# Stores on GpSimd's queue, late sums in single steps, five early down steps, and each product's high parts first, in a layer of HGRN2, RWKV-7 and a ConvFFN

## The chip, the cores and the metric

One core of a Trainium2 chip runs the whole layer. The metric is the device time of one execution in microseconds; the median of the runs counts.

## The reference

Input and output are (1, 2048, 1024) in float32. The layer, cut to what matters:

```python
h = _rmsnorm(x, norm1_w)
proj = h @ w_in                                  # 1024 -> HGRN2 and RWKV-7 columns
o_hg = _hgrn2_mixer(...); o_rw = _rwkv7_mixer(...)
x = x + concat([o_hg, o_rw]) @ w_out
u = _rmsnorm(x, norm2_w) @ w_up                  # 1024 -> 2 * 2816
u = causal_depthwise_conv(u, width=3) + conv_b
gate, val = split(u, 2)
x = x + (silu(gate) * val) @ w_down              # 2816 -> 1024
return _rmsnorm(x, final_norm_w)
```

The change lies behind the two mixers: in the end of the output projection, the up projection, and the down projection.

## The kernel before

The time axis (2048) is cut into four blocks of 512. **Stage 1** runs norm, input projection, both mixers and most of the output projection. **Stage 2** begins at about 1390 us of the span and has three parts.

*Operands in two parts.* Each float32 operand is split into a high and a low part: ScalarE (ACT) casts (L245 in `split`, L238 in `split_to`), VectorE (DVE) subtracts (L246, L239). A product is three matmuls of 128x128 by 128x512 in `mm3` (L261 high by high, L262 and L263 with a low part each), summed in one PSUM bank. In the names, a final h or l is the part: `uwh`, `uwl`, `Bh`, `Bl`, `dah`, `dal`.

*The end of the output projection (1390 to 1440 us, tile `wacc`).* The last block, two halves of 512 columns with eight steps `n` of four tiles each. The results are added to the residual and stored to `x1d` in DRAM (SP's queue). Beside it the first operands of the up stage are built: `br` tiles are loaded and split into `Bh`, `Bl`.

*The up stage (1440 to 2338 us, tiles `ua`, `ub`, `ud`).* The up product uses seven products of half-size blocks instead of eight, so sums of operands are needed on both sides: of weights (`weight_sums`), of activations (`Ts`), for the down stage of its weights (`Tw`) and of its inputs (`Sg`). The function `run` goes over 44 iterations n, 22 (`NFF`) for each half h of the time axis. An iteration has seven calls of `prod`, each 12 matmuls: a11, a12, s2, s1, s3, and a22 and s4, which run late, within the next iteration. ACT copies three sums out of PSUM as `m` (L117, `part`), and `ua` can't be written again before; DVE finishes the columns (convolution, gate, `y`) and SP stores them to `gd` (L1447). At the end of the first half, `between` adds one product of the down stage (tile `fa`, 11 steps of 12 matmuls), a step behind most calls of `prod` in n = 21 and 22.

*Side jobs.* `side` is a list of small jobs in a written order; `aside(n)` takes one after each product, if the job's first iteration (`first_at`) has come. `norm_last` normalizes the second half's blocks, `four` makes four sums of four loaded `br` tiles (a ring of six): load, nothing, two operations, two operations and four stores, nothing. For `Sg` of the second group (g = 1) the kk-th set starts at iteration 35 + kk, 8 of 11 sets (`EARLY`); the other three are made in the down stage by `g_sums`.

*The down stage (2338 to 2731 us, tiles `da`, `db`).* 143 steps (g, p, kk) of 12 matmuls. The first three are made at the up stage's end by `down_start`, called between the last s4 product and the rest of `late`, with `br`/`uw` tiles; then a new pool opens, whose operands `draw` are loaded by `load`, four steps ahead, and split by `take`, two ahead. Residual tiles of 512 KB (`xt`, L1473) and the last norm's weights (`fw`) are loaded in between. Finished rows go out to `out` (L1489).

A list scheduler orders each engine's instructions; the order below is its result, before and after. DMAs are issued by SP or by GpSimd (POOL): each is a queue with an order of its own, in which a transfer that waits for its data holds up those behind it.

Of the kernel before, what the change touches and what calls it, by code (L numbers as in the profile page):

```python
# [18 lines left out]
P = 128  # L19
# [42 lines left out]
def tile_layer(ctx, tc, consts, x, norm1_w, w_in, hg_lb_logits, hg_norm_w, rw_shift_mu, rw_w0, rw_w2,  # L62
# [5 lines left out]
    dma = nc.sync.dma_start  # L68
# [112 lines left out]
    EARLY = 8  # L181
# [10 lines left out]
    def g_sums(tile_, g, kk):  # L192

        a11, a12, a21, a22 = (tile_(krows(gd_[2 * g + u], q, kk)) for u in range(2) for q in range(2))
        V.tensor_add(a22, a21, a22)
        V.tensor_sub(a21, a11, a21)
        V.tensor_sub(a11, a22, a11)
        V.tensor_sub(a12, a12, a11)
        for i, t_ in enumerate((a22, a11, a21, a12)):
            dma(krows(Sg[g][i], 0, kk), t_)  # L200
# [7 lines left out]
    def d_loads(s_, tile_):  # L208
        g, p, kk = steps[s_]
        _, a, b = DP[p]  # L210
        return (tile_(krows(Sg[g][a], 0, kk) if isinstance(a, int) else krows(gd_[2 * g + a[0]], a[1], kk)),
                tile_(krows(Tw[b], 0, kk) if isinstance(b, int) else wd_quarter(*b, kk)))

# [45 lines left out]
    def mm3(acc, lhs, rhs, first, last, skip=False):  # L259
        (lh, ll), (rh, rl) = lhs, rhs  # L260
        TE.matmul(acc, lh, rh, start=first, stop=False, skip_group_check=skip)  # L261
        TE.matmul(acc, lh, rl, start=False, stop=False, skip_group_check=skip)  # L262
        TE.matmul(acc, ll, rh, start=False, stop=last, skip_group_check=skip)  # L263

# [843 lines left out]
    with ExitStack() as c2:  # L1108
# [36 lines left out]
        with tc.tile_pool(name="op", bufs=1, reuse_waits="tile") as op_:  # L1145
# [52 lines left out]
            for dh in range(2):  # L1198
                accs = [pst("wacc") for _ in range(4)]
                for n, k in enumerate((0, 1, 4, 5, 2, 3, 6, 7)):  # L1200
                    w = weights(k, dh)
                    if dh == 0:
                        take(k)
                    if n == 5:
                        for i in range(4):
                            t0 = b * BLK + i * P
                            if dh:
                                x_tile(i)
                            load(xt[i], x[0, t0:t0 + P, dh * 512:dh * 512 + 512])
# [12 lines left out]
                    for i in range(4):  # L1222
                        is_ = slice(i * P, (i + 1) * P)
                        mm3(accs[i], (ohl[k][0][:, is_], ohl[k][1][:, is_]), w, n == 0, n == KD - 1)
                for i in range(4):
                    V.tensor_add(xt[i], accs[i], xt[i])
                    dma(x1d[b][i * P:(i + 1) * P, dh * 512:dh * 512 + 512], xt[i])


        with tc.tile_pool(name="up", bufs=1, reuse_waits="tile") as up:  # L1230
# [11 lines left out]
            def norm_last(b, i2):  # L1242
# [11 lines left out]
                def evict(k, tp, w):  # L1254
                    t_ = hr.tile([P, 256], F32, tag="br", name="h2", bufs=6)
                    act(t_, tp, AF.Copy, scale=w)
                    dma(h2d[b][k * P:(k + 1) * P, i2 * 256:i2 * 256 + 256], t_)
# [4 lines left out]
            def four(srcs, make, dsts):  # L1262

                ts = []
                aside_of([lambda: ts.extend(raw_(v) for v in srcs), None,
                          lambda: make(ts, 0), lambda: (make(ts, 1), [dma(d, t_) for d, t_ in dsts(ts)]), None])
# [10 lines left out]
            def s_make(ts, part):  # L1277
                a11, a12, a21, a22 = ts
                if part == 0:
                    V.tensor_add(a22, a21, a22)  # L1280
                    V.tensor_sub(a21, a11, a21)
                else:
                    V.tensor_sub(a11, a22, a11)
                    V.tensor_sub(a12, a12, a11)
# [3 lines left out]
            s_out = lambda row: lambda ts: [(row(i), ts[j]) for i, j in enumerate((3, 0, 2, 1))]  # L1288
# [21 lines left out]
            def down_start():  # L1310

                accs = [pst("da") for _ in range(4)]
                raws = [d_loads(s_, raw_) for s_ in range(3)]
                for s_ in range(3):
                    lhs, rhs = (split(uw, t_, [P, BLK], "uw", 5) for t_ in raws[s_])
                    for i in range(4):
                        d_matmuls(accs, s_, lhs, rhs, i)
                dstate["accs"] = accs

            def between():  # L1320

                accs = [pst("fa") for _ in range(4)]
                for kk in range(KH):
                    lhs, rhs = (split(uw, raw_(v), [P, BLK], "uw", 5)
                                for v in (krows(gd_[0], 1, kk), wd_quarter(1, 0, kk)))
                    for i in range(4):
                        mm3(accs[i], [t_[:, i * P:(i + 1) * P] for t_ in lhs], rhs, kk == 0, kk == KH - 1, True)
# [3 lines left out]
                for i in range(4):  # L1331
                    t_ = raw_(None)
                    act(t_, accs[i], AF.Copy)
                    dma(M2[i], t_)
# [9 lines left out]
            def run():  # L1344
# [9 lines left out]
                for n in range(2 * NFF + 1):  # L1354
                    h, fb = n // NFF, n % NFF
                    if n < 2 * NFF:
# [7 lines left out]
                        def prod(acc, nm, bi, first, n=n, ops=ops):  # L1364
# [4 lines left out]
                            for k in range(4):  # L1369
                                mm3(acc, (wh[:, k, :], wl[:, k, :]), (bh[:, k, :], bl[:, k, :]),  # L1370
                                    first and k == 0, k == 3, True)
# [26 lines left out]
                    if n == 2 * NFF:  # L1398
                        break
# [22 lines left out]
                    def late(h=h, fb=fb, operand=operand, prod=prod, acc_a=acc_a, acc_d=acc_d, a22=a22, a12=a12, cg=cg,  # L1422
# [23 lines left out]
                        for b in range(2):  # L1446
                            (dma if end is None else nc.gpsimd.dma_start)(gd_[2 * h + b][fb * P:(fb + 1) * P, :],  # L1447
# [5 lines left out]
    with tc.tile_pool(name="dn", bufs=1, reuse_waits="tile") as dn:  # L1453
# [11 lines left out]

        def load(s_):
# [18 lines left out]
        def finish(g, u, i):  # L1485
# [3 lines left out]
            dma(out[0, t0:t0 + P, :], t_)  # L1489
# [16 lines left out]
        for s_ in range(3, 7):  # L1506
            load(s_)
        take(3)
        take(4)
# [3 lines left out]
        for s_ in range(3, N):  # L1513
# [6 lines left out]
            if s_ < N - 3:  # L1520
                lhs, rhs = ops.pop(s_)
                for i in range(4):
                    d_matmuls(acc, s_, lhs, rhs, i)
                    if kk == KH - 1:
# [50 lines left out]
```

## Time and profile before

| | us |
|---|---|
| runs | 2748.82, 2748.41, 2739.77 (median 2748.41) |
| profiled execution | 2740.67 |
| its span | 2738.9 |
| TensorE busy in the span | 2634.9 (96%) |
| VectorE, ScalarE, GpSimd busy | 1896.9, 1344.5, 367.4 |

A row of waits reads: engine, line and tile that waited, the engine, tile and line it waited for, us in total, times, longest. A row of DMA issues: out<-in, queue, number, KB each, median us from issue to landing. A row of the timeline: start, length, engine, line, operation, out<-in. A matmul's length is modelled and overlaps the next one's, so the pace is read from the starts. PE is TensorE, SPq and POOLq are the queues of SP and GpSimd.

### The profile page before, as it was taken

Reading aid. Unit: us, or ns where it says so; the run is one execution under the profiler, and the core shown is the slowest. Engines: PE = TensorE matmul, PEld = TensorE weight load, DVE = VectorE, ACT = ScalarE, POOL = GpSimd, SP = SyncE. Lnnn points to the kernel's source line nnn. Section 1 sums busy time; section 2 is a strip of 40 time slices with the busy share of each in tenths; the row PEclk is TensorE's granted clock in tenths of the full one; section 3 lists DMA queues with packets and bytes.
Section 4 is the critical chain, followed back from the end, with each engine's and each line's share of the span. In section 5 each row is a group of like instructions: output and inputs, shape, how many; then the busy total and the mean of one; then the engine's idle time right before and its main releaser. Section 6 shows DMA issues by size and latency. Waiting matters only on the chain.

```text
span 2738.9 us, 47949 instructions
## 1 busy us (share of the span) xinstructions
PE 2634.9 (96%) x18059; PEld 2098.9 (77%) x18059; DVE 1896.9 (69%) x3665; ACT 1344.5 (49%) x2168; POOL 367.4 (13%) x660
## 2 busy tenths in 40 slices
PE   7999999989999999999899999999999999999998
PEld 6777777767777767777677788887888877788887
DVE  4857656566556664656667889988898888667556
ACT  5446443444544444334456754556545444445444
POOL 6433222212321113222100000000000000000000
PEclk9999999999999999999999999999999999999999
DMA  8655544355663546844575357746763454888665
GB/s 302 200 159 165 165 138 128 115 152 164 216 189 105 152 137 208 273 142 133 168 260 179 118 197 265 237 151 208 259 223 123 145 185 151 285 303 273 214 193 185
DMA packets 365438, 517.87 MB, mean 189 GB/s; under 512 B 97440, under 2 KB 194070, under 8 KB 365206
## 3 DMA queue, kind: packets, MB, share of 16 engines
q1 hardware_dynamic: 313265, 345.39, 39.3%
q0 software_dynamic: 51872, 169.41, 19.0%
q8 instruction: 142, 2.33, 0.3%
q14 instruction: 91, 0.74, 0.1%
q10 hardware_dynamic: 68, 0.02, 0.0%
HBM read 376.27 MB, written 138.41 MB: 188 GB/s over the span
## 4 chain that ended last, share of the span: by engine, by line
PE 67%; DMA 10%; DVE 10%; issue 6%; ACT 4%; SPq 1%; POOL 1%; DVEq 0%; ACTq 0%; POOLq 0%
PE pj L261 8%; PE pj L262 7%; PE pj L263 7%; PE ua L261 4%; PE ua L263 4%; PE ua L262 4%; PE da L262 2%; PE da L261 2%; PE da L263 2%; PE ud L263 2%; PE ud L261 2%; PE ud L262 2%; PE db L262 2%; PE db L263 2%; PE hg L972 2%
## 5 line engine op out<-in xcount | busy, mean ns | idle before, releaser
L261 PE MATMUL pj<-hh,wh 128*128 128x512 f32 x960 | 403.2, 420 | 2.3 <-ACT hh L117 1.4
L263 PE MATMUL pj<-hh,wl 128*128 128x512 f32 x960 | 380.0, 396 | 0.1
L262 PE MATMUL pj<-hl,wh 128*128 128x512 f32 x960 | 379.1, 395 | 0.0
L261 PE MATMUL ua<-Bh,uwh 128*128 128x512 f32 x704 | 277.0, 393 | 10.4 <-ACT m L117 9.3
L263 PE MATMUL ua<-Bh,uwl 128*128 128x512 f32 x704 | 274.5, 390 | 0.1
L262 PE MATMUL ua<-Bl,uwh 128*128 128x512 f32 x704 | 274.2, 390 | 0.0
L261 PEld LDWEIGHTS pj<-hh,wh 128*128 128x128 f32 x960 | 181.7, 189 | 55.4 <-issue 12.7
L263 PEld LDWEIGHTS pj<-hh,wl 128*128 128x128 f32 x960 | 181.5, 189 | 40.8 <-DMA wl<-Win170l 0.9
L262 PEld LDWEIGHTS pj<-hl,wh 128*128 128x128 f32 x960 | 181.8, 189 | 39.6 <-issue 6.2
L245 ACT CAST uwh<-uraw 128x512 fp32r<-128x512 f32 x220 | 133.2, 616 | 101.5 <-PE ua L262 42.0
L246 DVE TENSOR_TENSOR dal<-draw,dah 128x512 fp32r<-128x512 f32 x140 | 96.7, 690 | 116.0 <-ACT dah L245 115.4
L245 ACT CAST dah<-draw 128x512 fp32r<-128x512 f32 x140 | 87.1, 622 | 169.9 <-PE da L262 81.6
L246 DVE TENSOR_TENSOR uwl<-uraw,uwh 128x512 fp32r<-128x512 f32 x220 | 146.8, 686 | 31.3 <-ACT uwh L245 31.1
L261 PEld LDWEIGHTS ua<-Bh,uwh 128*128 128x128 f32 x704 | 132.2, 188 | 41.8 <-ACT m L117 14.0
L263 PEld LDWEIGHTS ua<-Bh,uwl 128*128 128x128 f32 x704 | 132.2, 188 | 28.7 <-DVE uwl L246 1.0
L262 PEld LDWEIGHTS ua<-Bl,uwh 128*128 128x128 f32 x704 | 132.3, 188 | 26.6
L261 PE MATMUL ud<-Bh,uwh 128*128 128x512 f32 x352 | 137.8, 391 | 0.0
L263 PE MATMUL ud<-Bh,uwl 128*128 128x512 f32 x352 | 137.1, 389 | 0.0
L262 PE MATMUL ud<-Bl,uwh 128*128 128x512 f32 x352 | 137.0, 389 | 0.0
L261 PE MATMUL da<-dbh,dah 128*128 128x512 f32 x340 | 131.2, 390 | 3.4 <-ACT dbh L245 3.4
L262 PE MATMUL da<-dbl,dah 128*128 128x512 f32 x340 | 132.5, 390 | 0.5 <-DVE dbl L246 0.5
L263 PE MATMUL da<-dbh,dal 128*128 128x512 f32 x340 | 132.1, 389 | 0.0
(570 smaller groups left out, 6049.5 us busy)
## 6 DMA issues: line engine op xcount, KB each, us to landing
uraw<-in_w_up_dram SPq DMA_DIRECT2D x176, 256.0 KB, 3.2
woraw<-in_w_out_dram POOLq DMA_DIRECT2D x96, 256.0 KB, 3.6
br<-gd SPq DMA_DIRECT2D x90, 256.0 KB, 4.4
draw<-Sg SPq DMA_DIRECT2D x88, 256.0 KB, 3.2
draw<-Tw SPq DMA_DIRECT2D x88, 256.0 KB, 3.5
gd<-y SPq DMA_DIRECT2D x86, 256.0 KB, 3.0
Sg<-br SPq DMA_DIRECT2D x76, 256.0 KB, 2.5
xt<-x1d SPq DMA_DIRECT2D x32, 512.0 KB, 6.7
```

The source lines that it names most:

```text
L245: S.copy(hi, src)
L246: V.tensor_sub(lo, src, hi.bitcast(F32))
L261: TE.matmul(acc, lh, rh, start=first, stop=False, skip_group_check=skip)
L262: TE.matmul(acc, lh, rl, start=False, stop=False, skip_group_check=skip)
L263: TE.matmul(acc, ll, rh, start=False, stop=last, skip_group_check=skip)
L972: TE.matmul(o, kt[:, t0:t0 + 64], qs, start=True, stop=True, tile_position=(0, e * 64))
```

## The change

Four edits. (1) `store` is GpSimd's queue: the stores of x1d, h2d, Ts, Tw, Sg, gd, M2 and the first group's output move there from SP's, 286 in all; SP's program goes from 1339 to 1053 instructions and GpSimd's from 664 to 950. (2) The sums `Sg` have seven jobs: load, two empty, then one operation and its store each; the second group's sets start at iteration 36 + kk, and 7 of them instead of 8 are made in the up stage. (3) `down_start` makes five steps (`DS`) instead of three, and loads each step's operands in turn, not all ahead; the residual loads of p = 0 move from kk = 4, 6, 8, 10 to 5, 6, 8, 9. (4) `terms3` orders 12 matmuls as four high by high, then four of each low part, in `prod`, `between`, the down steps but each p's last, and the first two of the eight steps of the projection; before, each tile's three followed one another. TensorE's and VectorE's numbers of instructions stay as they were.

```diff
-    dma = nc.sync.dma_start
+    dma, store = nc.sync.dma_start, nc.gpsimd.dma_start
...
-    EARLY = 8
+    DS = 5
+    EARLY = 7
...
+    def terms3(jobs, first, last):
+
+        for j in range(3):
+            for n, (acc, (lh, ll), (rh, rl)) in enumerate(jobs):
+                TE.matmul(acc, *((lh, rh), (lh, rl), (ll, rh))[j], start=first(n) and j == 0, stop=last(n) and j == 2,
+                          skip_group_check=True)
...
-                    dma(x1d[b][i * P:(i + 1) * P, dh * 512:dh * 512 + 512], xt[i])
+                    store(x1d[b][i * P:(i + 1) * P, dh * 512:dh * 512 + 512], xt[i])
...
+            def sums(g, kk):
+
+                ts = []
+                ops = ((3, V.tensor_add, 2, 3), (2, V.tensor_sub, 0, 2), (0, V.tensor_sub, 3, 0), (1, V.tensor_sub, 1, 0))
+
+                def op(d, f, a, b, i):
+                    f(ts[d], ts[a], ts[b])
+                    store(krows(Sg[g][i], 0, kk), ts[d])
+
+                aside_of([lambda: ts.extend(raw_(krows(gd_[2 * g + u], q, kk)) for u, q in QB), None, None]
+                         + [lambda o=o, i=i: op(*o, i) for i, o in zip((0, 2, 1, 3), ops)])
+
             for g in range(2):
-                for kk in range(({0: KH, 1: EARLY})[g]):
-                    first_at[0] = NFF + 1 + g * (KH + 1 + kk)
-                    four([krows(gd_[2 * g + u], q, kk) for u, q in QB], s_make,
-                         s_out(lambda i, g=g, kk=kk: krows(Sg[g][i], 0, kk)))
+                for kk in range((KH, EARLY)[g]):
+                    first_at[0] = NFF + 1 + g * (KH + 2 + kk)
+                    sums(g, kk)
...
-                raws = [d_loads(s_, raw_) for s_ in range(3)]
-                for s_ in range(3):
-                    lhs, rhs = (split(uw, t_, [P, BLK], "uw", 5) for t_ in raws[s_])
-                    for i in range(4):
-                        d_matmuls(accs, s_, lhs, rhs, i)
+                for s_ in range(DS):
+                    lhs, rhs = (split(uw, t_, [P, BLK], "uw", 5) for t_ in d_loads(s_, raw_))
+                    d_step(accs, s_, lhs, rhs)
...
-                            (dma if end is None else nc.gpsimd.dma_start)(gd_[2 * h + b][fb * P:(fb + 1) * P, :],
+                            store(gd_[2 * h + b][fb * P:(fb + 1) * P, :],
...
-                if p == 0 and kk in (4, 6, 8, 10) or p == 2 - g and kk in (1, 3, 5, 7):
-                    u, i = (0, kk // 2 - 2) if p == 0 else (1, kk // 2)
+                if p == 0 and kk in XT or p == 2 - g and kk in (1, 3, 5, 7):
+                    u, i = (0, XT.index(kk)) if p == 0 else (1, kk // 2)
```

**VectorE, in one iteration of the late sums (g = 1).** The additions and subtractions of `br` tiles are the four operations of a set (L1280 to L1284 before, L1308 after); `uwl` are low parts of weights, `y`, `cg`, `cv` the finishing of columns. Before:

```order
L246 TENSOR_TENSOR uwl_22111<-s1_22086,uwh_22110 128x512
L1280 TENSOR_TENSOR br_22013<-br_22011,br_22013 128x512
L1281 TENSOR_TENSOR br_22011<-br_22007,br_22011 128x512
L246 TENSOR_TENSOR uwl_22134<-uraw_21986,uwh_22133 128x512
L1283 TENSOR_TENSOR br_22007<-br_22013,br_22007 128x512
L1439 SCALAR_TENSOR_TENSOR y1_22057<-cv_21895,cvt_14639,y1_22057 128x1024
L1431 TENSOR_TENSOR cg_21894<-ud_21897,m2_21937 128x512
L1440 SCALAR_TENSOR_TENSOR y1_22057<-cv_21895,cvt_14639,y1_22057 128x1024
L1284 TENSOR_TENSOR br_22009<-br_22009,br_22007 128x512
```

After, from the last operation of one set to the third of the next:

```order
L1434 TENSOR_TENSOR cv_21716<-ud_21718,m3_21791 128x512
L1308 TENSOR_TENSOR br_21822<-br_21822,br_21820 128x512
L1451 COPY cg_21878<-halo_15086 128x2
L1451 COPY cv_21879<-halo_15086 128x2
L252 TENSOR_TENSOR uwl_21922<-s1_21899,uwh_21921 128x512
L1308 TENSOR_TENSOR br_22067<-br_22065,br_22067 128x512
L1308 TENSOR_TENSOR br_22065<-br_22061,br_22065 128x512
L252 TENSOR_TENSOR uwl_21941<-uraw_21799,uwh_21940 128x512
L1308 TENSOR_TENSOR br_22061<-br_22067,br_22061 128x512
L1454 SCALAR_TENSOR_TENSOR y1_21870<-cv_21716,cvt_14639,y1_21870 128x1024
```

The first operation stays at the same place of an iteration, while the last one stands 21 rows behind the first instead of 4 to 7, in the next iteration.

**TensorE, at the end of the up stage.** `ud` is the last s4 product, `da` with `uw` operands the early down steps, `da` with `dbh`, `dah` the first step from the new pool. Before, there are 31 early matmuls from the last `ud` to that step, of which these rows are the first and the last:

```order
L263 MATMUL ud<-Bh_15084,uwl 128x512
L263 MATMUL da<-uwh,uwl 128x512
L261 MATMUL da<-uwh 128x512
L262 MATMUL da<-uwl,uwh 128x512
```

```order
L263 MATMUL da<-uwh,uwl 128x512
L261 MATMUL da<-dbh,dah 128x512 x4
```

After, 14 rows of four stand there, 56 matmuls; the first six of them and the row ahead:

```order
L275 MATMUL ud<-Bh_15084,uwl 128x512 x4
L275 MATMUL da<-uwl,uwh 128x512 x4
L275 MATMUL da<-uwh,uwl 128x512 x4
L275 MATMUL da<-uwh 128x512 x4
L275 MATMUL da<-uwl,uwh 128x512 x4
L275 MATMUL da<-uwh,uwl 128x512 x4
L275 MATMUL da<-uwh 128x512 x4
```

Two more steps stand ahead of the new pool's first operand, and the parts come in fours.

**ScalarE, in the first iteration of the up stage.** `m1` is the copy that frees `ua`; the casts to `Bh6`, `Bh2` wait for loads of `br`, the one to `uwh` for a load of weights (`uraw`). Before:

```order
L238 CAST Bh5_14664<-br_15137 128x512
L117 ACTIVATE m1_15153<-ua_15088 128x512
L238 CAST Bh6_14658<-br_15159 128x512
L238 CAST Bh6_14658<-br_15163 128x512
L238 CAST Bh6_14658<-br_15167 128x512
L238 CAST Bh6_14658<-br_15171 128x512
L117 ACTIVATE m2_15216<-ua_15088 128x512
```

After:

```order
L244 CAST Bh5_14664<-br_15137 128x512
L244 CAST Bh6_14658<-br_15167 128x512
L244 CAST Bh6_14658<-br_15171 128x512
L244 CAST Bh2_15084<-br_15188 128x512
L251 CAST uwh_15260<-uraw_15251 128x512
L117 ACTIVATE m1_15153<-ua_15088 128x512
L244 CAST Bh2_15084<-br_15192 128x512
```

`m1` moves behind four casts of `Bh6` (two stand just ahead of these rows), one of `Bh2` and one of weights.

More of the change, by code (lines that the diff above doesn't have):

```diff
@@ L212, in d_loads, with d_step @@
                 tile_(krows(Tw[b], 0, kk) if isinstance(b, int) else wd_quarter(*b, kk)))
+    def d_step(accs, s_, lhs, rhs):
+        g, p, kk = steps[s_]
+        terms3([(accs[i], [t_[:, i * P:(i + 1) * P] for t_ in lhs], rhs) for i in range(4)],
+               lambda i: kk == 0 and p in (0, 1, 3), lambda i: False)
     def d_matmuls(accs, s_, lhs, rhs, i):
@@ L1488, in finish @@
             t0 = (2 * g + u) * BLK + i * P
-            dma(out[0, t0:t0 + P, :], t_)
+            (dma if g else store)(out[0, t0:t0 + P, :], t_)
         def evict(g, p, accs, i):
@@ L1505, in tile_layer @@
         accs = {"a": dstate["accs"]}
-        for s_ in range(3, 7):
+        for s_ in range(DS, DS + 4):
             load(s_)
-        take(3)
-        take(4)
+        take(DS)
+        take(DS + 1)
         fw = dn.tile([P, D], F32, name="fw")
@@ L1512, in tile_layer @@
         sums_at = {KH + 6 * j + 2: EARLY + j for j in range(KH - EARLY)}
-        for s_ in range(3, N):
+        for s_ in range(DS, N):
             g, p, kk = steps[s_]
@@ L1521, in tile_layer @@
                 lhs, rhs = ops.pop(s_)
[L1522 to L1524 removed]
+                if kk < KH - 1:
+                    d_step(acc, s_, lhs, rhs)
+                else:
+                    for i in range(4):
+                        d_matmuls(acc, s_, lhs, rhs, i)
                         evict(g, p, accs, i)
```

37 lines of the change are left out of this document (16 added, 21 removed).

## The prediction

> **What bounds the kernel now.** I read the page first, then the busy time by stretches, then TensorE's waits in each stretch, then the queues behind those waits.
>
> ```profile
> span 2738.9 us, 47949 instructions
> PE 2634.9 (96%) x18059; PEld 2098.9 (77%) x18059; DVE 1896.9 (69%) x3665; ACT 1344.5 (49%) x2168; POOL 367.4 (13%) x660
> ```
>
> TensorE is busy nearly throughout. Stage 1 (to about 1390 us) keeps its order of instructions on every engine, so only what lies behind it can move.
>
> ```profile
> core 0: us, PE busy (x) PEld busy (x) DVE busy (x) ACT busy (x) POOL busy (x), PEclk, DMA share, GB/s
> 1390.00:1440.00 50.00, 47.55 (x203) 38.58 (x202) 36.47 (x59) 25.06 (x43) 0.63 (x1) 0.97 0.91 304
> 1440.00:2338.00 898.00, 882.53 (x3898) 723.22 (x3897) 771.04 (x1168) 492.21 (x752) 0.00 (x0) 1.00 0.58 188
> 2338.00:2731.00 393.00, 388.95 (x1708) 319.70 (x1707) 245.63 (x369) 188.01 (x341) 1.10 (x2) 1.00 0.73 242
> 1560.00:1700.00 140.00, 140.00 (x630) 115.27 (x629) 122.69 (x194) 78.33 (x124) 0.00 (x0) 1.00 0.65 213
> 2191.00:2331.00 140.00, 133.01 (x579) 108.25 (x580) 115.94 (x169) 66.76 (x100) 0.00 (x0) 1.00 0.52 169
> ```
>
> The rows are the last block's output projection, the up stage, the down stage, a clean piece of the up stage and its late piece. The granted clock is full from 1440 us on. TensorE stands still for 2.45 us in the first, 15.47 in the second and 4.05 in the third, 22.0 together; in the clean piece not at all. Its pace where nothing waits:
>
> ```profile
> 1619.69 0.39 PE L261 MATMUL ua<-Bh,uwh 128*128 128x512 f32 x1
> ...
> 1622.18 0.39 PE L263 MATMUL ua<-Bh,uwl 128*128 128x512 f32 x1
> 1622.41 0.39 PE L261 MATMUL ud<-Bh,uwh 128*128 128x512 f32 x1
> ...
> 1624.90 0.39 PE L263 MATMUL ud<-Bh,uwl 128*128 128x512 f32 x1
> ```
>
> 24 starts, 23 steps, 5.21 us: 0.2265 us from matmul to matmul, though each lasts 0.39 (they overlap). The step from L263 to L261 at 1622.18, where weights, moving operand and accumulator all change, is 0.23 like the others. So the second half of the change, another order of the same matmuls, has no pace to win or lose; it can only move the moment at which an operand is needed. And a wait costs more than the idle time shown, since the last matmul's end (0.39) was counted as busy where 0.23 would have done: idle time plus 0.16 a wait. The waits, for the output projection, for 1395 to 2340 us, and for 2340 to 2740:
>
> ```profile
> PE wacc L263 <- DVE Bl L239: 1.3, 1, 1.3
> PE wacc L262 <- DVE wol L239: 1.1, 1, 1.1
> ```
>
> ```profile
> PE ua L261 <- ACT m L117: 9.3, 8, 1.7
> PE fa L262 <- DVE uwl L246: 3.0, 2, 1.9
> PE fa L261 <- ACT uwh L245: 1.0, 1, 1.0
> PE ua L261 <- ACT uwh L245: 1.0, 1, 1.0
> PE tp L255 <- DVE xt L1252: 1.0, 1, 1.0
> ```
>
> ```profile
> PE da L261 <- ACT dbh L245: 3.4, 3, 1.5
> PE da L262 <- DVE dbl L246: 0.5, 2, 0.2
> PE db L262 <- DVE dbl L246: 0.2, 1, 0.2
> ```
>
> They add up to 2.4 + 15.3 + 4.1 = 21.8 us in 21 waits; with 21 x 0.16 = 3.4 that is **25 us, the most that stage 2 can give** without taking matmuls out, and the instruction counts are unchanged.
>
> **The change part by part.**
>
> *The late sums (7.1 us of the 9.3).* From 2185 to 2336 us the waits of TensorE, VectorE and SP's queue are
>
> ```profile
> PE ua L261 <- ACT m L117: 7.1, 6, 1.6
> ```
>
> ```profile
> DVE br L1280 <- DMA br<-gd: 19.0, 6, 3.9
> ```
>
> ```profile
> SPq L1447 <- DVE y L1445: 25.3, 8, 16.5
> SPq L1266 <- DVE br L1280: 23.4, 6, 4.7
> SPq L1266 <- DVE br L1284: 9.3, 3, 3.1
> ```
>
> Read from the bottom: SP stands 58 us at stores whose data aren't there; the loads of br behind them, which wait for gd besides, go out late; VectorE stands 19.0 us at the first sum with its other work queued behind; ACT's copy m comes late, and the next product on ua waits. The change cuts this in three places: the stores leave SP; the sums of the second group start one iteration later (84 matmuls, 19.0 us); and the four operations get a slot each, the last one 21 rows behind the first in VectorE's order instead of 4 to 7. Nothing then stands between br's landing and its use but the ring of six buffers: 6 x (1.18 + 0.16) = 8.1 us. I take **8.0**; bounds 0 and 8.1. One set fewer is done here and one more in the down stage, where VectorE is free a third of the time (245.63 of 393 busy).
>
> *Stores, price.* Landing times, all at 256 KB:
>
> ```profile
> gd<-y SPq DMA_DIRECT2D x86, 256.0 KB, 3.0
> Sg<-br SPq DMA_DIRECT2D x76, 256.0 KB, 2.5
> gd<-y POOLq DMA_DIRECT2D x2, 256.0 KB, 4.2
> Win171h<-wh POOLq DMA_DIRECT2D x1, 256.0 KB, 9.1
> ```
>
> The same store is 1.2 us slower on GpSimd's queue; a store on that queue took up to 9.1 us in stage 1. GpSimd waits for data there in SP's stead, with only stores behind it, and it is busy 0.00 and 1.10 us in the up and down stages, so nothing else waits for it. Cost 0 as long as buffers come free in time; what it costs otherwise is the second rival. Here the Trainium skill speaks against the change: "SBUF — State Buffer", sections "SBUF: two separate sides" (the box on the trap) and "Summary: rules for kernel authors", says that GpSimd's queue has its descriptors made in software, which VectorE's two-port modes starve (620 ns become 3100 there). VectorE is busy 86% of the up stage (771.04 of 898), but the page also finds two-input additions harmless, which most of it is; no run here shows the effect yet. With each store 2.5 us longer, an estimate from that page, the sum would move toward the second rival.
>
> *Output projection (2.4).* Four tiles' high products first, for the first two of eight steps: a low part is needed after 4 or 8 matmuls instead of 1 or 2, so 0.9 to 1.8 us instead of 0.23 to 0.45. The waits of 1.1 and 1.3 go to about 0.4 and 0. I take **2.2**, with the 0.16s; bounds 0 and 2.7.
>
> *The extra product fa (4.0 in three waits, 4.5 with the rest).* The same delay of the low parts, by 0.7 and 1.4 us, meets waits of 1.9 and 1.1 us; the wait of 1.0 for a high part isn't touched by it, but the weights' loads no longer stand behind stores. **3.0**; bounds 0 and 4.5.
>
> *Start of the down stage (2.4 in 4 waits: both of the 0.5 at dbl, and of the 3.4 at dbh, from 2336 to 2366 us)*
>
> ```profile
> PE da L261 <- ACT dbh L245: 1.9, 2, 1.5
> ```
>
> Behind the last ud product stand 56 matmuls of early down steps now and 31 before: 12.7 us instead of 7.0 in which to open the new pool, load, cast and subtract. 5.7 us more cover than a wait of 1.5: gone, 2.4 + 0.6 = **3.0**. What comes late next is ACT's casts for the two added steps, four casts ahead of the last activation; four take 2.25 us (in the row of 1453.13, below) beside 24 matmuls, 5.4 us. Bounds 1 and 3.0, for a load of 512 KB that now sits elsewhere in SP's row.
>
> *The rest of the down stage (1.7 in 2 waits).* The four sums left there (three before) keep their stores on SP. **0.5**; bounds -2 and 2.
>
> *The rest of the up stage.* Of the 9.3 us at m, 2.2 are early: 1.7 at 1736 us and 0.5 at 1477, behind loads that queue after stores: **2.0** with the 0.16s. Against it stands the first iteration. On ACT before:
>
> ```profile
> 1442.08 0.59 ACT L117 ACTIVATE m<-ua 128x512 f32<-128x512 f32 x1
> 1446.62 2.62 ACT L238 CAST Bh<-br 128x512 fp32r<-128x512 f32 x4 [3.94 <-DMA br<-Ts]
> ...
> 1453.13 2.25 ACT L245 CAST uwh<-uraw 128x512 fp32r<-128x512 f32 x4 [0.38 <-DMA uraw<-in_w_up_dram]
> ```
>
> In the new order six casts that wait for loads (four of Bh6, one of Bh2, one of uraw) stand ahead of m, which the third product needs at about 1444.3 us. The loads go out earlier, since four x1d stores have left SP:
>
> ```profile
> 1438.96 2.11 SPq L1227 DMA_DIRECT2D x1d<-xh  x4
> ```
>
> If they land 4 us earlier than 1446.6, m runs at about 1446 and TensorE waits some 2 us; if they land as before, uraw at 1453, it waits 9. The waits for uwh and xt behind it (1.0 + 1.0) may go. **0** in all; bounds -7 and +2.
>
> Sum: 8.0 + 2.2 + 3.0 + 3.0 + 0.5 + 2.0 + 0 = 18.7 us. Of the profiled execution's 2740.67 us, 2722 stay. Its span (2738.9) is 1.8 shorter than its time. The three timed runs are 2748.82, 2748.41 and 2739.77: they lie in two groups 8.6 us apart, and the profiled one belongs to the lower. The median shown sits in the upper, from which the sum gives 2729.7. I forecast **2724**, nearer the one that the trace describes.
>
> **The rivals.**
>
> *The stalls move.* Loads on SP wait for the ring of br until a store on the slower queue lands, and the sums' wait stays by half, and fa's too. For it: SP already waited for Sg's landing, and the sums now hold their buffers through four slots. Against: the load for the next set's first operand has two spare buffers, and a set has 19 us. Gain 18.7 - 4 - 1.5 - 2 = 11: 2730 from the profiled run, 2737 from the median, so within half a per cent.
>
> *Slower: stores that land late hold up the up stage.* Place: the ring of br, 18 iterations with sums (11 of the first group, 7 of the second). The last of a set's stores goes out a product (2.7 us) into the next iteration, whose first sum comes three products after that, so 8 us hold the store, the load (4.4 at the median) and SP's issue; the loads of uraw stand behind in SP's row. A store of 3.6 us just fits; one of 9.1, as in the worst row above, is 5.5 late, some of it caught by VectorE's slack. At 3 us each, 18 x 3 = 54, less the 18.7: 2776. It decides from 2.1 us an iteration on (a landing of about 5.7): below that the loss doesn't lift the time half a per cent over the median.
>
> ```profile
> br<-gd SPq DMA_DIRECT2D x90, 256.0 KB, 4.4
> ```
>
> For it: 286 stores on a queue whose stores reached 9 us. Against: gd's own stores, at 4.2 us there, stay under the 5.7.
>
> *It does nothing.* The pace of matmuls was never the limit, as shown, and if what ends the waits is the landing of loads, not SP's row, both halves are worth little: 2738 to 2748. Here the Trainium skill's page "DMA: Bandwidth & Descriptors", section "Issuing engines are not separate DMA queues", fits: another engine as issuer saves only the issue itself, it says, since all share the same DMA engines. The trace agrees only in part: what SP loses are 58 us of waiting, not of issuing, and the DMA share is 0.52 in the late piece.
>
> **How the numbers follow.** Forecast 0.60 (own range 2712 to 2734), stalls that move 0.22 (2730 to 2740), nothing 0.09 (2738 to 2748), slower 0.09 (2760 to 2780). The range 2707 to 2744 takes in the first two and part of the third, and at its low end the whole 25 us and 9 us of an unseen gain at the upper end of the spread. Half a per cent of 2748, 13.7 us, is about what a measurement of this kernel can tell from no change. The first case lies over it but for its upper edge, the second and third within: faster 0.62, same 0.29, slower 0.09.
>
> **What would show it.** TensorE's idle time from 2191 to 2331 us falls from 7.0 to under 1, and VectorE's wait for br<-gd is gone from there; a wait of ua for m stands near 1444 us; no wait of da for dbh near 2346; fa's waits under 1.5; matmuls step by 0.2265 still. A landing of Sg or gd on GpSimd's queue over 5 us, with uraw late behind it, would make me wrong upward; a pace other than 0.2265 in either direction would show that the order of products does matter.

## The result, and the profile after

The change made the kernel slower: 2752.43 us against 2743.68 (medians of 22 runs each), ratio 1.0031, 95% interval 1.0020 to 1.0042. The forecast was 2724 us, with a range of 2707 to 2744, and 0.09 for slower by over half a per cent; what came is within half a per cent, on the slower side. The 22 runs put the kernel before 4.7 us under the median of three runs that was shown.

The page of the changed kernel, and its stages by their own bounds (last block's output projection, up stage, down stage; the columns are those of the table of stretches above):

```profile
span 2742.1 us, 48219 instructions
PE 2640.9 (96%) x18059; PEld 2102.6 (77%) x18059; DVE 1896.5 (69%) x3665; ACT 1360.2 (50%) x2168; POOL 522.2 (19%) x946
```

```profile
1388.40:1435.10 46.70, 45.23 (x194) 35.60 (x194) 33.70 (x57) 22.55 (x40) 2.25 (x5) 1.00 0.91 315
1435.10:2344.70 909.60, 885.86 (x3897) 726.33 (x3897) 769.60 (x1166) 502.31 (x754) 139.34 (x258) 0.99 0.57 183
2344.70:2734.40 389.70, 389.05 (x1714) 320.79 (x1712) 248.44 (x373) 195.13 (x342) 14.00 (x26) 1.00 0.74 253
```

By the starts of the matmuls (first wacc, last wacc, last ud, last of all) the same stages took 48.2, 898.2 and 394.1 us before. So the projection gained 1.5 us and the down stage 4.4, about as forecast, and the up stage lost 11.4. The loss lies in the up stage. TensorE's waits there, and in the down stage:

```profile
PE ua L275 <- ACT m L117: 16.7, 12, 4.1
PE fa L275 <- DVE uwl L252: 2.7, 2, 1.8
PE fa L275 <- ACT uwh L251: 2.2, 1, 2.2
PE tp L261 <- DVE xt L1268: 2.0, 1, 2.0
```

```profile
PE da L275 <- DVE dbl L252: 0.7, 2, 0.4
```

The down stage's waits went from 4.1 to 0.7 us. The wait of ua for m, 9.3 us before, is 16.7. It sits in three places.

*The first iteration.* ScalarE, where m stands behind the casts, as the order said:

```profile
1441.76 0.62 ACT L244 CAST Bh<-br 128x512 fp32r<-128x512 f32 x1 [0.73 <-DMA br<-Ts]
1442.70 0.62 ACT L244 CAST Bh<-br 128x512 fp32r<-128x512 f32 x1 [0.32 <-DMA br<-h2d]
1443.94 0.62 ACT L251 CAST uwh<-uraw 128x512 fp32r<-128x512 f32 x1 [0.62 <-DMA uraw<-in_w_up_dram]
1444.46 0.59 ACT L117 ACTIVATE m<-ua 128x512 f32<-128x512 f32 x1
```

The stage itself began 3.7 us earlier in this span (last wacc at 1435.1, before at 1438.8), so the times are counted from there. The loads did land early (uraw's cast at 8.8 us instead of 14.3), yet m came at 9.4 us instead of 3.3, and TensorE stood from 1441.0 to 1445.1. What that cost behind it, four stretches of the same trace:

```profile
1436.00:1440.50 4.50, 4.50 (x21) 3.72 (x21) 4.39 (x8) 3.15 (x7) 1.34 (x3) 1.00 0.90 292
1441.00:1444.50 3.50, 0.00 (x0) 0.00 (x0) 3.36 (x7) 1.83 (x5) 0.38 (x1) 0.84 0.92 308
1445.10:1450.00 4.90, 4.90 (x12) 3.83 (x13) 1.95 (x4) 1.66 (x3) 0.00 (x0) 0.50 1.07 361
1452.00:1456.00 4.00, 4.00 (x20) 3.30 (x18) 3.92 (x9) 3.17 (x7) 0.00 (x0) 1.00 0.60 185
```

PEclk, the third column from the right, falls to 0.50 after the standstill: 12 matmuls start in 4.9 us, 0.41 each, where 0.23 is the pace.

*The sums Tw, 1690 to 1727 us.* From 1660 to 1810 us TensorE, VectorE and SP's queue waited

```profile
PE ua L275 <- ACT m L117: 5.1, 4, 2.3
```

```profile
DVE br L1288 <- DMA br<-in_w_down_dram: 7.5, 4, 3.4
DVE br L1287 <- DMA br<-in_w_down_dram: 3.4, 2, 1.7
```

```profile
SPq L1136 <- DMA Tw<-br: 57.3, 32, 5.6
```

SP, rid of the stores, arrives early at the next loads of br and waits there for stores to land: 57.3 us in 32 waits, where the kernel before had 12.1 in 12 in this piece. Before, TensorE lost some 2 us there.

*The late sums.* Nothing was won, from 2190 to 2345 us:

```profile
PE ua L275 <- ACT m L117: 7.5, 7, 1.6
```

```profile
DVE br L1308 <- DMA br<-gd: 18.4, 5, 5.0
```

19.0 us of VectorE's wait became 18.4, though no store stands in SP's row any more. SP stands at loads of weights instead, whose buffers VectorE has to free; in the same stretch, before and after:

```profile
SPq L1140 <- DVE uwl L246: 26.5, 12, 6.7
SPq L1153 <- DVE uwl L252: 61.5, 11, 7.3
```

The forecast's chain was read right from TensorE to VectorE and wrong behind it.

### The profile page after: what moved, and what is told of

Read it like the earlier page. It is cut to its first block, busy times and chain, and to the rows that moved or that the text cites. A ratio compares the mean times of both kernels' runs of the same rounds, so it can differ in the third digit from the quotient of the medians.

```text
span 2742.1 us, 48219 instructions
## 1 busy us (share of the span) xinstructions
PE 2640.9 (96%) x18059; PEld 2102.6 (77%) x18059; DVE 1896.5 (69%) x3665; ACT 1360.2 (50%) x2168; POOL 522.2 (19%) x946
## 4 chain that ended last, share of the span: by engine, by line
PE 69%; DMA 10%; DVE 9%; issue 7%; ACT 3%; POOL 1%; SPq 1%; DVEq 0%; POOLq 0%; ACTq 0%
PE ua L275 11%; PE pj L267 8%; PE pj L268 7%; PE pj L269 7%; PE da L275 7%; PE ud L275 6%; PE db L275 5%; PE ub L275 3%; PE hg L985 2%; DMA br<-in_w_down_dram 2%; DVE uwl L252 1%; DMA woraw<-in_w_out_dram 1%; PE rw L721 1%; DVE y L1454 1%; PE rw L901 1%
## 5 line engine op out<-in xcount | busy, mean ns | idle before, releaser
L275 PE MATMUL ua<-Bh,uwh 128*128 128x512 f32 x704 | 192.5, 395 | 16.7 <-ACT m L117 16.7
L275 PE MATMUL ua<-Bl,uwh 128*128 128x512 f32 x704 | 190.0, 392 | 0.0
L275 PE MATMUL ua<-Bh,uwl 128*128 128x512 f32 x704 | 189.8, 392 | 0.0
L1462 POOL DMA_DIRECT2D gd<-y x88 | 47.5, 544 | 473.2 <-DVE y L1460 429.5
L251 ACT CAST wh<-woraw 128x512 fp32r<-128x512 f32 x96 | 59.0, 618 | 108.0 <-DMA woraw<-in_w_out_dram 49.2
L251 ACT CAST uwh<-s 128x512 fp32r<-128x512 f32 x88 | 53.8, 620 | 113.2 <-DVE s L1356 78.4
L252 DVE TENSOR_TENSOR dbl<-draw,dbh 128x512 fp32r<-128x512 f32 x138 | 95.0, 688 | 20.0 <-ACT dbh L251 20.0
L251 ACT CAST dbh<-draw 128x512 fp32r<-128x512 f32 x138 | 86.0, 623 | 44.3 <-DMA draw<-in_w_down_dram 13.1
L316 DVE SCALAR_TENSOR_TENSOR rkv<-pj,vt,rkv 128x511 f32<-128x511 f32 x48 | 35.9, 747 | 98.2 <-ACT rkv L117 98.2
```

What stands on the lines that cost most here:

```text
L251: S.copy(hi, src)
L252: V.tensor_sub(lo, src, hi.bitcast(F32))
L275: TE.matmul(acc, *((lh, rh), (lh, rl), (ll, rh))[j], start=first(n) and j == 0, stop=last(n) and j == 2, skip_group_check=True)
L316: V.scalar_tensor_tensor(y[:, 1:], acc[:, :BLK - 1], mu, y[:, 1:], ALU.mult, ALU.add)
L1462: store(gd_[2 * h + b][fb * P:(fb + 1) * P, :], ys[0][:, b * BLK:(b + 1) * BLK])
```

## Experiments

Times are ratios to the kernel before on the same chip, with 95% intervals; two kernels are compared by the quotient of their ratios, whose interval is about ±0.002. "Excess" is worked out from the starts of the matmuls: each step over 0.236 us counts with what it has over 0.2267. The pieces are the first 40 us behind the last wacc, the Tw sums (from 180 us behind it to the first fa), fa, and the late piece (behind fa); the 140 us between the first 40 and the Tw sums are left out, where the excess is 4.2 to 5.7 us in most kernels and 6.6 to 7.5 in three. One profiled execution each.

| kernel | ratio | first 40 | Tw | fa | late | up stage | down stage |
|---|---|---|---|---|---|---|---|
| before, 1st and 2nd profile | 1 | 2.3, 4.1 | 2.0, 1.7 | 5.5, 8.4 | 9.4, 11.5 | 898.2, 904.7 | 394.1, 394.4 |
| changed, 1st and 2nd | 1.0031, 1.0029 | 6.8, 7.7 | 8.2, 7.6 | 5.7, 7.2 | 9.5, 10.3 | 909.6, 912.4 | 389.7, 389.2 |
| stores on SP | 0.9967 | 1.3 | 0.2 | 5.1 | 5.3 | 891.4 | 394.4 |
| x1d on SP | 1.0005 | 2.1 | 5.6 | 6.6 | 6.5 | 900.3 | 388.9 |
| old sums | 1.0055 | 6.4 | 6.2 | 7.0 | 16.2 | 917.9 | 389.0 |
| stores on SP, old sums | 0.9978 | 1.8 | 0.0 | 7.0 | 6.5 | 894.7 | 391.2 |
| only gd on GpSimd | 1.0010 | 2.1 | 5.9 | 7.4 | 8.4 | 904.2 | 392.5 |
| x1d and gd on SP | 0.9999 | 2.3 | 7.0 | 5.6 | 6.6 | 901.0 | 389.0 |
| stores on SP, ring 5 | 1.0007 | 2.2 | 3.9 | 13.0 | 5.0 | 904.0 | 394.1 |
| down stage's stores on GpSimd | 0.9969 | 1.2 | 0.0 | 6.0 | 7.9 | 894.2 | 389.2 |
| x1d on SP, ring 7, 1st and 2nd | 0.9979, 0.9989 | 0.7, 0.8 | 7.7, 5.9 | 3.9, 4.0 | 9.8, 11.7 | 901.7, 904.2 | 389.3, 391.0 |
| down stage's stores, ring 7 | 0.9958 | 1.8 | 2.0 | 4.4 | 8.1 | 895.6 | 389.7 |
| order of products only | 0.9978 | 0.4 | 0.0 | 5.8 | 7.7 | 893.0 | 394.1 |
| five early steps only | 0.9988 | 1.4 | 1.6 | 8.1 | 10.1 | 900.1 | 390.5 |
| order, x1d on GpSimd | 1.0003 | 7.6 | 0.9 | 6.5 | 8.3 | 901.9 | 391.4 |
| Sg's loads on GpSimd too | 1.0026 | 8.6 | 6.4 | 7.6 | 13.1 | 915.3 | 389.0 |
| Ts/Tw loads on GpSimd too | 1.0030 | 1.8 | 16.4 | 7.0 | 8.1 | 915.6 | 389.5 |

**All moved stores back on SP.**

```diff
-    dma, store = nc.sync.dma_start, nc.gpsimd.dma_start
+    dma, store = nc.sync.dma_start, nc.sync.dma_start
```

The two stores of gd that the kernel before already has on GpSimd's queue stay there.

> All moved stores go back to SP's queue; new sums, five early steps and the order of products stay. Theory (the stores on GpSimd's queue make the up stage longer): the wait of ua for m near 1441 us goes, the half clock behind it too, and those from 1690 to 1727 us mostly; from the last matmul on wacc to the last on ud 898 us instead of 909.6, the kernel 11 us under the changed one and 0.1 to 0.3% under the one before. Rival (the new sums or the order of products cost it): the up stage stays over 905 us and the time within 4 us of the changed kernel's.

0.9967 (0.9951 to 0.9983), up stage 891.4 us: the theory held, by more than it asked. The stores alone cost the changed kernel 1.0031/0.9967 = 0.64%, 17.5 us; everything else in it is a gain of 0.33%, 9 us. SP's wait for Tw's landing is back at

```profile
SPq L1136 <- DMA Tw<-br: 10.5, 14, 2.6
```

**Only x1d back on SP.**

```diff
-                    store(x1d[b][i * P:(i + 1) * P, dh * 512:dh * 512 + 512], xt[i])
+                    dma(x1d[b][i * P:(i + 1) * P, dh * 512:dh * 512 + 512], xt[i])
```

> Only the eight x1d stores go back to SP's queue. Theory (ACT's order puts the copy m behind casts that wait for loads, because the scheduler thinks that the loads are early once x1d has left SP): m stands ahead of those casts, the wait of 4.3 us at 1441 us and the seven us of half clock behind it go, some 6 us in all; the up stage takes 903 us instead of 909.6. Rival (the casts, not the order, are what is late): the wait moves to the fourth or fifth product and the up stage stays over 907.

The excess of the first 40 us fell from 6.8 to 2.1, m stands ahead of the casts again (4.2 us behind the last wacc), and 0.26% came back. The rest of the stores' cost stays, with 5.6 us at the Tw sums.

**The reverse: the order of products and x1d alone on GpSimd's queue.** The first of these kernels is the one before with `terms3`; the second adds

```diff
-                    dma(x1d[b][i * P:(i + 1) * P, dh * 512:dh * 512 + 512], xt[i])
+                    nc.gpsimd.dma_start(x1d[b][i * P:(i + 1) * P, dh * 512:dh * 512 + 512], xt[i])
```

> The kernel before with the new order of products alone. Theory (the order changes when a low part is needed, and nothing of TensorE's pace): output projection 46 to 46.7 us instead of 48.15, up stage within 3 us of 898, down stage within 2 of 394; 0 to 3 us faster. Rival (the order shifts the other engines' orders enough to matter): the up stage off by more than 3 us.

> The kernel before with the new order of products and, of the stores, the eight of x1d alone on GpSimd's queue. Theory (these stores by themselves put m behind casts on ACT): the wait of 4 us at the third product of the up stage and half the clock behind it are there, 4 to 7 us of excess in the first 40 us of the up stage instead of 0.4; 5 to 8 us slower than the kernel with the order alone. Rival (the stall needs the other stores too): excess under 3 us there, no difference in time.

The order alone: 0.9978 (0.9965 to 0.9991), 6 us faster. The projection took 46.3 us, as expected, but the up stage fell by 5.2, more than the 3 I allowed, in one profile: its excess goes down in the first 40 us, at the Tw sums and late, and not at fa. With x1d's stores on GpSimd's queue 0.25% are gone again, at the place named:

```profile
PE ua L275 <- ACT m L117: 4.9, 1, 4.9
```

There m comes 10.0 us behind the last wacc. Taking these stores out of the changed kernel and putting them into another one give the same 7 us, each with an error of some 5, and the same standstill goes and comes with them: this mechanism is shown.

**Old sums, with the stores on GpSimd's queue and on SP's.** `sums` and its place go back to `four` with `s_make`, `EARLY` to 8; in the second, `store` is SP's too.

```diff
-                    first_at[0] = NFF + 1 + g * (KH + 2 + kk)
-                    sums(g, kk)
+                    first_at[0] = NFF + 1 + g * (KH + 1 + kk)
+                    four([krows(gd_[2 * g + u], q, kk) for u, q in QB], s_make,
+                         s_out(lambda i, g=g, kk=kk: krows(Sg[g][i], 0, kk)))
```

> The sums Sg are made as before (two pairs of operations in four slots, eight sets early, one iteration sooner), the rest of the change stays. Theory (the late sums' wait comes from loads that stand in SP's row behind weights' loads which wait for VectorE, so how the sums are spread does little): TensorE's excess from 2190 to 2310 us within 3 us of the 9 of both kernels, the time within 4 us of the changed kernel's. Rival (the later start and single steps did help, and something else took it back): the late piece gets 5 us or more longer.

> Stores on SP and sums as before: what stays of the change is the order of products and the five early down steps. Theory (these two are the good part): the output projection 1.5 us shorter, the down stage 4 us shorter, the up stage as before within 2 us; 5 to 7 us under the kernel before, 0.2%. Rival (the order of products harms the up stage): the up stage 3 us or more over its 898.

With stores on GpSimd's queue the late piece got 6.7 us longer (16.2), and the time 0.24%, as the rival said. The new sums did help there, and the stores had taken it back. With stores on SP the excess differs by 1.2 us (6.5 against 5.3), less than the 2.1 between two profiles of the kernel before. The second kernel did as its theory said in time (0.9978), with the up stage 3.5 under before.

**Which stores.** From the first experiment, gd alone on GpSimd's queue; from the second, gd back on SP, which leaves the stores of br tiles there.

```diff
-                            store(gd_[2 * h + b][fb * P:(fb + 1) * P, :],
+                            nc.gpsimd.dma_start(gd_[2 * h + b][fb * P:(fb + 1) * P, :],
```

> As the first experiment (all moved stores on SP), but the stores of gd from GpSimd's queue. Theory (what costs is that stores of br tiles land later, and so free the ring of six later; gd's tile isn't in that ring): the up stage 891 us within 2, as in the first experiment, the piece of the Tw sums without excess. Rival (any store on that queue costs, or what waits for gd's landing): 895 us or more.

> As the second experiment (x1d back on SP), with the stores of gd back on SP too, those of br tiles on GpSimd's queue. Theory (the ring of br, freed later by the slower queue): the excess of 5.6 us in the piece of the Tw sums stays, SP waits over 40 us for Tw's landing there, the up stage is about 900 us. Rival (the stores of br stand in GpSimd's row behind a store of gd that waits 8 us for y): the excess falls under 1 us and the up stage to about 893.

gd alone cost 0.43%, as the rival said. Its excess at the Tw sums is 5.9 us with Tw's stores on SP and 16.7 us of waiting for their landing; there the loads of br stand in SP's row behind stores that wait for VectorE:

```profile
SPq L1282 <- DVE br L1288: 11.6, 7, 2.5
SPq L1282 <- DVE br L1291: 7.8, 6, 2.5
```

With gd back on SP nothing is won (0.9999 against 1.0005): the excess of 7.0 and SP's wait are as its theory said.

```profile
SPq L1136 <- DMA Tw<-br: 56.0, 32, 5.5
```

So the two costs don't add up. Taking gd's stores out of SP's row, those of br tiles, or both gave the scheduler another row each time, and in each the loads of br came late, by different waits. With x1d's stores alone moved they did not (0.9 us at the Tw sums).

**The ring of br.** Five buffers with the stores on SP; seven with them on GpSimd's queue (room for the seventh from m3, which moves into m1's tile).

```diff
-            t_ = hr.tile([P, BLK], F32, tag="br", name="br", bufs=6)
+            t_ = hr.tile([P, BLK], F32, tag="br", name="br", bufs=7)
...
-                    m3 = part(acc_a, "m3")
+                    m3 = part(acc_a, "m1")
```

> As the first experiment (stores on SP), with a ring of five br buffers instead of six. Theory (the ring is the limit, so that a buffer that comes free later is the same as one buffer less): SP's wait for Tw's landing rises from 10.5 to over 40 us, TensorE's excess in the piece of the Tw sums to 4 us or more, the up stage to over 897. Rival (the ring has room to spare and the queue itself is what is slow): the up stage within 2 us of 891.

> As the second experiment (stores on GpSimd's queue but for x1d), with a ring of seven br buffers; the room comes from m3, which now shares m1's buffer. Theory (late landing of stores on GpSimd's queue costs through the ring of br): SP's wait for Tw's landing in the piece of the Tw sums falls from 59 to under 30 us, TensorE's excess there from 5.6 to under 2, the up stage from 900.3 to 896 or less, and the time by 4 to 6 us. Rival (SP's row, in which weights' loads and br's loads hold up each other, is what is late, whatever the ring): the up stage over 899.

> A second profiled execution of the ring of seven with stores on GpSimd's queue, whose times said 7 us less than with six while its profile said no less. If the ring is a limit: up stage 896 or less this time. If it isn't: 899 or more again, and the gain in time lies elsewhere.

Five cost 0.40%, and the up stage is over 897 us as expected, but not by the path named: most of it at fa (13.0), and SP waited 11.4 us for Tw's landing, not 40. Seven gained 0.26% in the first session and 0.16% in the second, where the error is 0.2 to 0.3%; neither profile shows less excess at the Tw sums (7.7, 5.9), and SP's wait there hardly falls, from 59.3 us:

```profile
SPq L1136 <- DMA Tw<-br: 51.6, 33, 6.3
```

With one buffer less the ring is a limit of the up stage, but one more is not what the Tw sums lack.

**Loads out of SP's row.** Two kernels issue the loads for the sums on GpSimd's queue too: those for Sg in the changed kernel, those for Ts and Tw in the one with x1d and gd on SP, as here.

```diff
+                def go():
+                    loader[0] = store
+                    ts.extend(raw_(v) for v in srcs)
+                    loader[0] = dma
```

> The changed kernel with the loads of the sums Sg from GpSimd's queue as well, where only stores stand. Theory (these loads are late because they stand in SP's row behind loads of weights that wait for VectorE to free a buffer): VectorE's wait for br<-gd from 2190 to 2345 us falls from 18.4 to under 8, TensorE's excess in the late piece from 9.5 and 10.3 to under 5, the kernel 4 us or more faster than the changed one. Rival (they wait for gd's and Sg's stores to land, in whatever row): the wait over 14, the excess over 8.

> As the kernel with x1d and gd on SP and the stores of br tiles on GpSimd's queue, with the loads for the sums Ts and Tw on that queue as well. Theory (the loads and the loads of weights hold up one another in SP's row): VectorE's wait for br in the piece of the Tw sums falls from 8.8 to under 3 us, TensorE's excess from 7.0 to under 2, the up stage from 901 to 896. Rival (the stores on that queue land too late, whoever loads): excess over 4.

Both came as the rivals said: in the first VectorE's wait for br<-gd is 20.8 us and the late excess 13.1, in the second the excess at the Tw sums is 16.4 and the time 0.31% longer. In a row without loads of weights the loads still wait for the stores of Tw (second kernel), and they stand behind stores that wait for VectorE (first kernel, late piece):

```profile
POOL br L1136 <- DMA Tw<-br: 22.2, 14, 3.2
POOL gd L1467 <- DVE y L1465: 80.1, 8, 18.0
```

So getting away from the weights' loads doesn't bring the loads of br earlier. That weights' loads cost nothing in SP's row is not shown by this, since the other row has waits of its own.

**The down stage.** Five early steps alone on the kernel before, and from the first experiment the down stage's stores alone on GpSimd's queue, the latter also with seven buffers.

```diff
-            store(krows(Sg[g][i], 0, kk), t_)
+            nc.gpsimd.dma_start(krows(Sg[g][i], 0, kk), t_)
...
-            (dma if g else store)(out[0, t0:t0 + P, :], t_)
+            (dma if g else nc.gpsimd.dma_start)(out[0, t0:t0 + P, :], t_)
```

> The kernel before with the five early down steps alone (and the residual loads moved). Theory (more cover for the new pool's first loads): down stage 390 to 391.5 us instead of 394, up stage 903.6 where two more steps of 5.4 us are... counted to the last ud product within 3 us of 898, as those steps stand behind it; 2 to 4 us faster. Rival (the cover is not what was lacking, and casts or loads for those steps come late): a down stage over 393.

> As the first experiment, with the stores of the down stage alone (the late sums Sg there and the first group's output) from GpSimd's queue. Theory (in the down stage no load waits for these stores, so there only the freed row of SP counts): down stage 389 us instead of 394, up stage 891 within 2, 5 us under the first experiment, 0.5% under the kernel before. Rival (the 394 of the first experiment were a chance of one execution): down stage within 2 us of 394 again, or no difference in time.

> As the kernel with the down stage's stores alone on GpSimd's queue, with the ring of seven. Theory (the ring is a limit with stores on SP too, as the ring of five showed): the up stage from 894 to 889 us, most of it in the pieces of fa and of the late sums; 0.4 to 0.6% under the kernel before. Rival (at six the ring has room enough there, and m3 in m1's buffer makes a new wait): within 3 us of 894 or above.

(In the first of these expectations the up stage is meant to be 898, counted to the last ud.) Five steps: 390.5 us instead of 394.1, in time 0.9988 (0.9971 to 1.0006), too little for its interval. The stores of the down stage on GpSimd's queue: 389.2 instead of the 394.4 of the first experiment, where da still waited 2.0 us for dbh once:

```profile
PE da L275 <- ACT dbh L251: 2.0, 1, 2.0
PE da L275 <- DVE dbl L252: 1.1, 2, 0.9
```

In time the two can't be told apart (0.9969 and 0.9967). With seven buffers 0.9958 (0.9939 to 0.9976) is the lowest ratio of all, 11.5 us under the kernel before and 20 under the changed one, though not to be told from the two others; its up stage of 895.6 was not the 889 expected.

**How far one profile goes.** Before and changed kernel were profiled once more.

> A second profiled execution of the kernel before. If stage lengths can be read from one execution: up stage 898 within 3 us, down stage 394 within 1, the excess of each piece within 1.5 us of the first time's. If not: off by 5 us or more, and only times can tell the up stages apart.

> A second profiled execution of the changed kernel. If the losses named are the kernel's own: again a wait of 4 us for m at the third product with the clock at half behind it, 6 to 9 us of excess in the piece of the Tw sums, up stage 906 to 913. If they were chance: one of the pieces is off by more than 3 us.

The changed kernel repeats its losses (6.8 and 7.7, 8.2 and 7.6 us). The kernel before doesn't repeat its up stage: 898.2 and 904.7, spread over the first 40 us, fa and the late piece. So a difference of 5 us between two up stages is not shown by one profile each, while the Tw piece and the down stage repeat within 0.6 us.

## Why the prediction was wrong, step by step

Several points rest on how late the stores on GpSimd's queue landed, in the changed kernel from 1400 to 2340 us:

```profile
gd<-y POOLq DMA_DIRECT2D x86, 256.0 KB, 2.6
Sg<-br POOLq DMA_DIRECT2D x72, 256.0 KB, 3.3
Tw<-br POOLq DMA_DIRECT2D x44, 256.0 KB, 3.8
x1d<-xh POOLq DMA_DIRECT2D x8, 256.0 KB, 6.9
```

On SP's queue before, the medians were 3.0, 2.5, 3.5 and 3.2, of those stores whose landing that trace shows.

- **The step that failed is the price of the stores**, "Cost 0 as long as buffers come free in time". They cost 0.64%, 17.5 us, about the 18.7 that the rest was to bring; without them the rest brings 9. The price went by two stores of gd that landed after 4.2 us; on the whole gd landed no later than before. The second rival named place and ring, but priced it by stores that land after 5.7 us and more, and no store of Tw or Sg took longer than that: none is slow enough by itself. x1d's eight took 5.7 to 8.3 us, but they don't stand in the ring, and what their landing costs, apart from the order that brings m late, is not shown. The Trainium skill, "SBUF — State Buffer", has 620 ns that become 3100 when VectorE starves GpSimd's queue. The trace does not bear out the 2.5 us more that I estimated from it for each store: Tw and Sg took 0.3 and 0.8 more and gd 0.4 less, while x1d took 3.7 more, and no run shows whether that is the reason.
- **The first iteration was put at 0 between -7 and +2; it was -4.5** against the kernel before (6.8 us of excess in the first 40 against 2.3), and -7 against the kernel with the order alone. The order showed m behind six casts, and the working took the loads at their best for the sum: m at 1446, 7.2 us behind the last wacc, and a wait of 2. It came at 9.4, TensorE stood 4.1 us, and the standstill halved the clock behind it. Of the two waits of 1.0 that I let go against it, uwh's went, and xt's, near 1556 us, grew to 2.0.
- **Late sums, 8.0: got 0.** I took SP's 58 us behind stores for the cause of VectorE's 19 us because both stood in the same stretch. With the stores gone from SP's row VectorE waited 18.4. Single steps and a later start were worth 6.7 us with the stores on GpSimd's queue, and on SP's no more than two profiles differ by.
- **Early waits near 1736 us, 2.0: became a loss of 6**, at the Tw sums, beside a wait for landing such as the first rival described. That rival was right in kind (0.22) and too mild.
- **Output projection, 2.2: 1.5** in this profile, 1.8 with the order alone, none in the second (48.3).
- **fa, 3.0: nothing** (5.5 to 5.7 us of excess). Low parts needed later do not help where a high part is late: its wait rose from 1.0 to 2.2.
- **Down stage, 3.5: 4.4**, and 3.5 for the five steps alone. The cover argument held there, but cover was not enough everywhere: the first experiment makes five steps too and took 394.4 us, with 2.0 of wait for dbh. With the old sums it was 391.2, and with the down stage's stores off SP's queue 389.2.
- **The pace of matmuls** is 0.2267 us in either order; that its order has no worth but through when operands are needed held, and this was worth 6 us, in other pieces than I named.

What stays open is why loads of br wait for their stores so much longer once these are on the other queue. Loading from GpSimd's queue, away from the weights' loads, doesn't cure it, nor does one more buffer, and medians of landing differ by 0.3 us for Tw and 0.8 for Sg. That the row itself, which the scheduler writes anew with every store that moves, decides it, as the kernel with gd alone suggests, is argued, not shown: the order can't be held fixed here while a queue changes.

## What to carry to other kernels

A store that is moved to a queue of its own doesn't only leave a row, it also rewrites the others: look in the new order for what now stands ahead of the copy that frees an accumulator, and price that at its worst. Time spent waiting in a queue is no loss until the engine that needs the data waits less without it; undo one queue's move at a time before crediting it. A standstill of TensorE can cost the clock as well; from 2.6 us on it always did here.

## What the runs showed of the hardware

- After standstills of 4.1 to 4.9 us the granted clock was 0.50 for 6.8 us, and 11 steps took 0.43 us each instead of 0.227: 2.2 us on top of the wait, in both profiles of the changed kernel and in the one with x1d alone on GpSimd's queue. With the old sums a standstill of 4.5 us was followed by 3.4 us of half clock only (1454.0 to 1457.4). The Trainium skill, "TensorE: Matmul & The Clock Gate", Part 1, gives half rate after an idle window of about 3.4 us; the trace agrees for these, with 3.4 us or twice that at half rate.
- Shorter standstills cost the clock too, but not each. Behind 1400 us, over all profiles here, half clock followed all 10 standstills of 2.6 us and more, 15 of the 49 between 1.75 and 2.6, and 1 of the 57 between 1.5 and 1.75. In the changed kernel a wait of 2.3 us near 1722 was followed by it (0.50 from 1723.3 to 1726.7), one of 2.2 at fa was not. What decides among these is not shown.
- Stage 1, with one and the same order of instructions in all kernels, ended (first wacc of the last block) between 1380.9 and 1401.5 us of the span. This alone is wider than most effects here, so stages have to be compared from their own start.
